# An MoE kernel on one core: turning the first block, the second half of the next up product and the gate are put ahead of the third block's branch and of five weight splits

## The chip, the cores and the metric

The kernel runs on one core of one Trainium2 chip. The time is the device time of one launch in microseconds (us); the kernel before took 2101.19 us in the median of 3 runs (2099.44, 2101.19 and 2105.92). One further execution was taken by the hardware profiler; all rows below are from it.

Names of engines: PE is TensorE's matmul, PEld its weight load, DVE is VectorE, ACT is ScalarE, POOL is GpSimd, and SP is the queue from which the weight transfers are issued. Each works through its instructions in order.

## The reference, cut to what matters

A trunk of two residual layers on 1024 tokens of width 1024, all in float32. Layer 0 mixes tokens with a convolution and an attention, layer 1 with a linear recurrence; neither is touched by the change. Behind each mixer stands a mixture of experts (MoE) with 16 experts, of which each token takes two:

```python
def moe(h2, router_w, router_b, w1, w3, w2):
    ...
    _, loc = lax.top_k(in_group, TOP_K)                  # two experts for each token
    ...
    def run_block(args):
        tok, g, e = args
        xb = h2[tok]                                     # a block of up to 128 tokens of expert e
        y = (jax.nn.silu(xb @ w1[e]) * (xb @ w3[e])) @ w2[e]
        return y * g[:, None]
    ...
    return jnp.zeros_like(h2).at[buf_tok].add(...)
```

w1 and w3 are 1024 x 512 for each expert (the two up products), w2 is 512 x 1024 (the down product). So each layer reads 16 x 6 MB of expert weights, whatever the tokens are.

## The kernel before, in words

**Precision.** Every matrix product is made in three passes. A float32 operand is split into a rounded high part and the rest, both in the matmul's float32 format, and hi x hi, hi x lo and lo x hi are accumulated in one bank (mm3, lines 260 to 264). A product with 128 rows of depth and 512 columns is thus three matmuls; "half of an up product" (four depth steps of eight) is 12 matmuls.

**The weight stream.** The class Ring (lines 60 to 121) brings the weights of the experts in quarters, 128 x 1024 float32 or 512 KB each. SP issues them (line 81) into five tiles named raw (NSTG, line 39). A quarter is then split: ACT copies its high part into a weight slot (line 252), DVE subtracts that from the quarter for the low part (line 253). The raw tile is free for the next issue when both are done. There are four weight slots of four quarters each. The order of the quarters is first w1 and w3 of expert 0, and then for each expert e: w1 of e+1, w2 of e, w3 of e+1. How many quarters are split at which place of the loop stands in one line:

```python
SPLITS = (1, 2, 2, 1, 0, 3, 3)
```

In the loop over expert e (from line 1336) these are: the first quarter of w2 of e (SPLITS[0]); its other three (SPLITS[5], taken ahead of the loop's first branch, emitted in rest_h3); then 2, 2 and 1, which are the four quarters of w3 of e+1 and the first of w1 of e+2 (SPLITS[1] to [3]: the five quarters of the change); and last the other three of w1 of e+2 (SPLITS[6], in second_half). The five quarters go into the slots that w1 and w3 of expert e have held; drop(e, 0) and drop(e, 1) give these slots back. The last reader of these slots is the third or fourth block, inside the branch of line 1410, so the splits wait until PE is past that branch, also where it is skipped.

**Blocks.** Expert e's tokens come as up to four blocks. The first has up to 128 tokens and is always worked. The second is worked where the expert has more: "narrow" with up to 64 further tokens, with a form that needs half the passes (line 1365), or "wide" (line 1355). The third and fourth follow in the branch of line 1410. The branches are taken by a register, some, loaded for each expert on ACT, DVE, PE and POOL (kind: one of five kinds of counts). Rows of tokens are gathered by POOL one and two experts ahead, and the results are scattered by POOL (line 1216).

**The order.** In the expert loops ACT, DVE, PE and POOL run what is written in the order in which it is written (MANUAL, line 43); the transfers on SP are issued where issue() is called, in reload behind the splits. For expert e the order before is:

1. the first half of the w3 product of the first block (h3); the next expert's tokens are turned (prep: transposes on PE, line 1227, copies on ACT, line 1228, subtractions on DVE, line 1229); one split;
2. the branch of the second block: turned tokens, then rest_h3 (second half of h3, the multiplication with the gate, three splits), then the wide or narrow products; without a second block rest_h3 alone;
3. gathers on POOL; the first half of the next expert's w1 product (up1, line 1409);
4. the branch of the third block (line 1410);
5. two splits (line 1420); mid(sF) (line 1421: the first block's gated product is turned by four transposes on PE, line 1245, two ACT copies, line 1247, and two DVE subtractions, line 1248); two splits (line 1422);
6. the second half of up1 and gate_in (lines 1424 and 1425; the gate is one ACT instruction, line 1274); one split (line 1426);
7. the first half of the down product (12 matmuls, line 1430) and its eviction by DVE (line 1256); then, in a branch, the second half with the last three splits, the scatter, and the down products of the further blocks.

A bank of the accumulator is shared between uses: the first half of the first block's down product uses ys[0], and the second half of the second block's uses it again, after DVE has evicted the first (second_half and the lines behind it).

Of the kernel before, what the change touches and what calls it, by code (L numbers as in the profile page):

```python
# [21 lines left out]
KC = D // P  # L22
# [101 lines left out]
class Trunk:  # L124
# [1063 lines left out]
    def moe(self, l):  # L1188
# [48 lines left out]
        def mid(h, ht, n=P, bank=None):  # L1237

            for q in range(2 if bank is None else 1):
                if bank is None:  # L1240
                    js, pt = (2 * q, 2 * q + 1), psX.tile([P, 2, P], F32, name="pht", tag="px")
                else:
                    js, pt = range(4), bank.rearrange("p (j n) -> p j n", j=4)
                for j in js:
                    nc.tensor.transpose(pt[:, j - js[0], 0:n], h[0:n, P * j:P * j + P], self.ident[0:n, 0:n])
                o = slice(js[0], js[-1] + 1)
                nc.scalar.activation(ht[:, 0, o, 0:n], pt[:, :, 0:n], AF.Copy)  # L1247
                nc.vector.tensor_tensor(ht[:, 1, o, 0:n], pt[:, :, 0:n], ht[:, 0, o, 0:n].bitcast(F32),  # L1248
                                        op=ALU.subtract)
# [17 lines left out]
        def up1(e, xt, ks, h1):  # L1267
            mm(h1, xt, weights(e, 0), ks)
# [3 lines left out]
        def gate_in(e, h1):  # L1272
            s = slF[e] = hw.tile([P, FF], F32, name="slF", tag="slF")
            nc.scalar.activation(s, h1, AF.Silu)
# [59 lines left out]
        for e in range(NE):  # L1334
# [71 lines left out]
            if more:  # L1406
                gather_R(e + 1)
                h1 = psH.tile([P, FF], F32, name="h1", tag="h1")
                up1(e + 1, xtF[e + 1], range(4), h1)
            with tc.If(some > 2, preferred_fallthrough_block=False):  # L1410
                prep(rowB, xtR, (r, ys[1]))
                with tc.If(pool_kind(e) > 3):
                    gather(idx[:, c0 + 3:c0 + 4], rowB)
                wide(hx[0])
                with tc.If(some > 3, preferred_fallthrough_block=False):
                    prep(rowB, xtR, (r, ys[1]))
                    wide(hx[1])
            drop(e, 0)
            drop(e, 1)
            split(SPLITS[1])  # L1420
            mid(sF, xt[:, 0])
            split(SPLITS[2])
            if more:
                up1(e + 1, xtF[e + 1], range(4, KC), h1)
                gate_in(e + 1, h1)
            split(SPLITS[3])
            y = rows.tile([P, D], F32, name="y", tag="y")
            gF = gsl[:, c0:c0 + 1]
# [365 lines left out]
```

## Time and profile before

| | |
|---|---|
| median of 3 runs | 2101.19 us (2099.44 to 2105.92) |
| the profiled execution | 2103.05 us; its span 2101.3 us, granted clock 0.937 in the mean |
| busy share of the span | PE 88%, PEld 68%, DVE 66%, ACT 46%, POOL 21% |
| experts of layer 0 | 687.5 to 1171.7 us of the span |
| experts of layer 1 | 1573.8 to 2077.5 us of the span |

Times in rows are microseconds of the span unless they are means, which are in nanoseconds. An engine that is not busy is idle for a reason that the trace infers: "<-DMA raw" means that it waited for a transfer into a tile named raw, "<-PEq L1410" that it waited for a branch or a wait of line 1410 on PE's instruction queue, "<-issue" that nothing that the trace shows held it. Some matmul records are missing from a trace, so counts of matmuls can be a few short. The experts are counted from 0 in each layer. In the trace the bodies of the branches show which expert has which blocks.

### The profile page before, as it was taken

How to read it: one execution, taken by the hardware profiler on the slowest of the kernel's cores; microseconds unless marked ns; L12 is line 12 of the kernel's file. 1: busy time of each engine (PE TensorE's matmuls, PEld its weight loads, DVE VectorE, ACT ScalarE, POOL GpSimd, SP SyncE). 2: the span in 40 equal slices, each digit the busy share in tenths (PEclk: the TensorE clock that was granted, in tenths of full speed). 3: DMA queues.
4: the chain of work that ended last, by engine and by line, in shares of the span. 5: the costliest groups of instructions: out<-in, count | busy, mean ns of one | idle time of the engine just before them, and what ended most of it. 6: DMA issues, size and time to landing. Idle time of an engine off the chain costs nothing. (4 is left out here: it accounts for less than half of the span.)

```text
span 2101.3 us, 27568 instructions
## 1 busy us (share of the span) xinstructions
PE 1850.1 (88%) x9612; PEld 1433.4 (68%) x9612; DVE 1391.2 (66%) x2030; ACT 956.3 (46%) x1332; POOL 432.0 (21%) x264
## 2 busy tenths in 40 slices
PE   5999998998985899989898599999958999887885
PEld 3788575666874677767676478877747777765664
DVE  4599676776679665776756555676785453787772
ACT  3211226665223544555544457782233342565550
POOL 1311104330323111111110232213240110111110
PEclk8999998999986999999999799999979999998897
DMA  8111104677423877897877511124244763999981
GB/s 313 45 57 41 40 1 139 224 260 229 156 99 122 272 227 218 260 305 249 276 212 226 179 33 53 46 71 161 91 150 171 194 203 114 281 307 322 289 286 24
DMA packets 103369, 364.86 MB, mean 174 GB/s; under 512 B 13680, under 2 KB 15024, under 8 KB 103088
## 3 DMA queue, kind: packets, MB, share of 16 engines
q1 hardware_dynamic: 91216, 319.29, 44.8%
q0 software_dynamic: 11776, 41.95, 9.1%
q8 instruction: 157, 2.57, 0.5%
q14 instruction: 124, 1.02, 0.2%
q10 hardware_dynamic: 96, 0.03, 0.0%
HBM read 322.40 MB, written 38.83 MB: 172 GB/s over the span
## 5 line engine op out<-in xcount | busy, mean ns | idle before, releaser
L253 DVE TENSOR_TENSOR wt<-raw,wt 128x1024 fp32r<-128x1024 f32 x384 | 458.7, 1222 | 130.1 <-ACT wt L252 116.5
L252 ACT ACTIVATE wt<-raw 128x1024 fp32r<-128x1024 f32 x384 | 396.9, 1059 | 197.8 <-DMA raw<-in_ex_w_dram 152.3
L262 PE MATMUL h<-wt,xtF 128*128 128x512 f32 x512 | 211.4, 413 | 10.9 <-PEq L1450 5.1
L263 PE MATMUL h<-wt,xtF 128*128 128x512 f32 x512 | 204.5, 399 | 9.5 <-issue 9.5
L264 PE MATMUL h<-wt,xtF 128*128 128x512 f32 x512 | 204.8, 400 | 0.9 <-DVE xtF L1229 0.8
L482 DVE SCALAR_TENSOR_TENSOR cacc<-u,vecs,cacc 128x1024 f32<-128x1024 f32 x116 | 149.5, 1289 | 3.3
L262 PE MATMUL yp<-wt,xtF 128*128 128x512 f32 x256 | 114.7, 448 | 35.9 <-ACT xtF L1247 31.9
L253 POOL TENSOR_TENSOR wl<-raw,wh 128x1024 fp32r<-128x1024 f32 x32 | 85.1, 2678 | 239.6 <-ACT wh L252 232.4
L262 PEld LDWEIGHTS h<-wt,xtF 128*128 128x128 f32 x512 | 98.3, 192 | 32.8 <-issue 10.2
L264 PEld LDWEIGHTS h<-wt,xtF 128*128 128x128 f32 x512 | 98.2, 192 | 30.7 <-issue 6.0
L264 PE MATMUL yp<-wt,xtF 128*128 128x512 f32 x256 | 111.7, 436 | 5.7 <-DVE xtF L1248 4.7
L263 PEld LDWEIGHTS h<-wt,xtF 128*128 128x128 f32 x512 | 98.4, 192 | 26.4 <-issue 7.3
L262 PE MATMUL pout<-wouth,ch 128*128 128x512 f32 x256 | 110.2, 431 | 3.8 <-ACT wouth L252 2.2
L263 PE MATMUL yp<-wt,xtF 128*128 128x512 f32 x256 | 110.2, 431 | 0.0
L1228 ACT ACTIVATE xtF<-pxt 128x512 fp32r<-128x512 f32 x64 | 35.0, 595 | 163.5 <-PE pxt L1227 148.1
L263 PE MATMUL pout<-woutl,ch 128*128 128x512 f32 x256 | 104.1, 407 | 4.0 <-DVE woutl L253 3.4
L264 PE MATMUL pout<-wouth,cl 128*128 128x512 f32 x256 | 103.5, 404 | 0.1
L1216 POOL DMA_INDIRECT xacc<-y,sidx x16 | 33.9, 2121 | 335.7 <-DVE y L1256 312.0
L1216 POOL DMA_INDIRECT out_dram<-y,sidx x16 | 33.8, 2114 | 325.6 <-DVE y L1256 325.6
L262 PEld LDWEIGHTS yp<-wt,xtF 128*128 128x128 f32 x256 | 54.5, 213 | 57.4 <-ACT xtF L1247 36.9
L1526 POOL DMA_INDIRECT xg<-h2d,idx x45 | 58.7, 1305 | 126.0 <-issue 45.5
L1229 DVE TENSOR_TENSOR xtF<-pxt,xtF 128x512 fp32r<-128x512 f32 x64 | 41.2, 685 | 55.8 <-ACT xtF L1228 55.8
(403 smaller groups left out, 4252.0 us busy)
## 6 DMA issues: line engine op xcount, KB each, us to landing
raw<-in_ex_w_dram SPq DMA_DIRECT2D x384, 512.0 KB, 6.0
raw<-in_mod_w_dram SPq DMA_DIRECT2D x96, 512.0 KB, 4.7
raw<-in_ev_w_dram SPq DMA_DIRECT2D x16, 512.0 KB, 4.3
raw<-in_od_in_dram SPq DMA_DIRECT2D x16, 512.0 KB, 5.3
h2d<-x SPq DMA_DIRECT2D x14, 512.0 KB, 2.6
xs<-in_x_dram SPq DMA_DIRECT2D x8, 512.0 KB, 7.7
raw<-in_ev_out_dram SPq DMA_DIRECT2D x8, 512.0 KB, 5.7
x<-in_x_dram SPq DMA_DIRECT2D x8, 512.0 KB, 4.4
```

What stands on the lines that cost most here:

```text
L252: nc.scalar.activation(hi, raw, AF.Copy)
L253: (lo_eng or nc.vector).tensor_tensor(lo, raw, hi.bitcast(F32), op=ALU.subtract)
L262: nc.tensor.matmul(out, ah, bh, start=start, stop=False)
L263: nc.tensor.matmul(out, ah, bl, start=False, stop=False)
L264: nc.tensor.matmul(out, al, bh, start=False, stop=stop)
L482: nc.vector.scalar_tensor_tensor(y if j < CW - 1 else acc[:, c, :], u[:, j:j + S], self.vec("ev_dw_w", 4 * j + c), y, op0=ALU.mult, op1=AL ...
L1216: nc.gpsimd.indirect_dma_start(out=xacc, out_offset=bass.IndirectOffsetOnAxis(ap=col, axis=0), in_=y[0:n], in_offset=None, compute_op=ALU.add)
L1228: nc.scalar.activation(xt[:, q, 0], px, AF.Copy)
L1229: nc.vector.tensor_tensor(xt[:, q, 1], px, xt[:, q, 0].bitcast(F32), op=ALU.subtract)
L1526: self.nc.gpsimd.indirect_dma_start(out=dst, out_offset=None, in_=self.h2d[l], in_offset=bass.IndirectOffsetOnAxis(ap=col, axis=0))
```

## The change

The call mid(sF) and, where there is a next expert, the second half of up1 and gate_in are moved from behind the branch of line 1410 and between the splits to the place directly behind the first half of up1, ahead of that branch. The splits of 2, 2 and 1 quarters, with their reloads, now stand together behind the branch and the two drops. Nothing else is changed; SPLITS, the slots, the five raw tiles and the order of the quarters stay. So on PE the branch of line 1410 and the third block's products now stand between the second half of up1 and the down product; on ACT the two copies of mid and the gate stand ahead of the five splits; on DVE the two subtractions of mid stand ahead of the five subtractions; and SP's five issues stand behind them as before.

```diff
@@ -1407,6 +1407,10 @@
                 gather_R(e + 1)
                 h1 = psH.tile([P, FF], F32, name="h1", tag="h1")
                 up1(e + 1, xtF[e + 1], range(4), h1)
+            mid(sF, xt[:, 0])
+            if more:
+                up1(e + 1, xtF[e + 1], range(4, KC), h1)
+                gate_in(e + 1, h1)
             with tc.If(some > 2, preferred_fallthrough_block=False):
                 prep(rowB, xtR, (r, ys[1]))
                 with tc.If(pool_kind(e) > 3):
@@ -1418,11 +1422,7 @@
             drop(e, 0)
             drop(e, 1)
             split(SPLITS[1])
-            mid(sF, xt[:, 0])
             split(SPLITS[2])
-            if more:
-                up1(e + 1, xtF[e + 1], range(4, KC), h1)
-                gate_in(e + 1, h1)
             split(SPLITS[3])
             y = rows.tile([P, D], F32, name="y", tag="y")
             gF = gsl[:, c0:c0 + 1]
```

## Rows read from the trace of the kernel before

**Rows 1.** From the page: busy time of each engine over the whole span, its share, and the number of instructions.

```profile
PE 1850.1 (88%) x9612; PEld 1433.4 (68%) x9612; DVE 1391.2 (66%) x2030; ACT 956.3 (46%) x1332; POOL 432.0 (21%) x264
```

**Rows 2.** Busy time by windows: the experts of layer 0, those of layer 1, expert 8 of layer 0, and experts 5 to 14 of layer 1. Columns: the window and its length; busy us of PE, PEld, DVE, ACT and POOL, each with its number of instructions; the granted clock of PE; the busy share of the DMA engines; GB/s.

```profile
687.50:1171.70 484.20, 433.88 (x1954) 343.22 (x1952) 308.37 (x349) 239.78 (x308) 71.89 (x45) 0.96 0.80 244
1573.80:2077.50 503.70, 447.06 (x1955) 355.81 (x1954) 308.94 (x342) 238.14 (x298) 69.97 (x42) 0.95 0.74 228
935.50:966.00 30.50, 29.33 (x144) 23.72 (x143) 20.27 (x24) 16.88 (x23) 3.31 (x2) 1.00 0.76 237
1814.80:2051.20 236.40, 199.22 (x842) 155.67 (x840) 181.07 (x191) 143.84 (x170) 35.79 (x20) 0.93 0.93 299
```

**Rows 3.** Instructions of single lines. The first row, by lines: the narrow second block's products (busy us, mean ns, idle before). The others, by source line: the shortest, middle and longest duration in ns, and the first and last start; L1355 is the gate of a wide block (into slR the second, into rowA the third and fourth), L1410 on PEldq the semaphore step on PE's queue where the branch of the third block is skipped.

```profile
L1365 PE MATMUL r<-wt,xtR 128*128 128x512 f32 x144 | 35.1, 395 | 0.1
...
L1355 ACT ACTIVATE slR<-r x4: 597/597/598, 801.9 to 1725.3; 128x512 f32<-128x512 f32 x4
L1355 ACT ACTIVATE rowA<-r x3: 597/598/599, 1607.6 to 1754.9; 128x512 f32<-128x512 f32 x3
...
L1410 PEldq EVENT_SEMAPHORE x30: 51/51/51, 696.4 to 2065.7; - x30
```

**Rows 4.** The table of waits over the whole span: the engine and line that waited, what for, total us, number, longest us.

```profile
ACT wt L252 <- DMA raw<-in_ex_w_dram: 152.3, 145, 4.2
...
ACT wt L252 <- PEq L1410: 35.9, 17, 7.8
PE yp L262 <- ACT xtF L1247: 31.9, 11, 6.4
```

**Rows 5.** The timeline of ACT and PE in expert 6 of layer 0, an expert with one block: start, duration, engine, line, operation, number; in brackets the idle time before it and what ended it.

```profile
896.30 1.06 ACT L252 ACTIVATE wt<-raw 128x1024 fp32r<-128x1024 f32 x1 [3.45 <-DMA raw<-in_ex_w_dram]
...
899.66 1.06 ACT L252 ACTIVATE wt<-raw 128x1024 fp32r<-128x1024 f32 x1 [2.31 <-DMA raw<-in_ex_w_dram]
...
900.63 0.64 ACT L1247 ACTIVATE xtF<-pht 128x256 fp32r<-128x256 f32 x2
901.04 0.65 PE L262 MATMUL yp<-wt,xtF 128*128 128x512 f32 x1 [4.97 <-ACT xtF L1247]
```

**Rows 6.** The timeline of ACT, PE and DVE in expert 8 of layer 0, which has a second block.

```profile
954.28 2.01 ACT L252 ACTIVATE wt<-raw 128x1024 fp32r<-128x1024 f32 x2 [1.60 <-PEq L1410]
954.89 0.63 PE L1245 MATMUL pht<-ident,slF 128*128 128x128 f32 x4 [0.74 <-PEq L1410]
956.20 0.64 ACT L1247 ACTIVATE xtF<-pht 128x256 fp32r<-128x256 f32 x2
957.88 0.39 PE L264 MATMUL h<-wt,xtF 128*128 128x512 f32 x1
958.11 0.40 PE L262 MATMUL yp<-wt,xtF 128*128 128x512 f32 x1
958.32 3.48 DVE L253 TENSOR_TENSOR wt<-raw,wt 128x1024 fp32r<-128x1024 f32 x3
958.87 0.58 ACT L1274 ACTIVATE slF<-h 128x512 f32<-128x512 f32 x1
961.72 0.74 DVE L1256 SCALAR_TENSOR_TENSOR y<-yp,gsl,g2r 128x512 f32<-128x512 f32 x1
970.23 0.75 DVE L1256 SCALAR_TENSOR_TENSOR rowB<-yp,gsl,g2r 128x512 f32<-128x512 f32 x1 [2.05 <-PE yp L264]
```

**Rows 7.** The timeline of ACT and PE at the ends of runs of one-block experts in layer 0: in expert 0 the last split ahead of the copies, the copies, and the first matmul of the down product; then the copies of the next tokens at the starts of experts 1, 8, 11 and 14.

```profile
702.21 1.06 ACT L252 ACTIVATE wt<-raw 128x1024 fp32r<-128x1024 f32 x1 [1.49 <-DMA raw<-in_ex_w_dram]
706.53 0.64 ACT L1247 ACTIVATE xtF<-pht 128x256 fp32r<-128x256 f32 x2
706.95 0.80 PE L262 MATMUL yp<-wt,xtF 128*128 128x512 f32 x1 [6.40 <-ACT xtF L1247]
719.27 1.10 ACT L1228 ACTIVATE xtF<-pxt 128x512 fp32r<-128x512 f32 x2 [3.94 <-PE pxt L1227]
937.94 1.09 ACT L1228 ACTIVATE xtF<-pxt 128x512 fp32r<-128x512 f32 x2 [2.84 <-PE pxt L1227]
1021.21 1.09 ACT L1228 ACTIVATE xtF<-pxt 128x512 fp32r<-128x512 f32 x2 [0.82 <-PE pxt L1227]
1120.06 1.09 ACT L1228 ACTIVATE xtF<-pxt 128x512 fp32r<-128x512 f32 x2 [3.40 <-PE pxt L1227]
```

**Rows 8.** Groups of instructions by line in the window of experts 5 to 14 of layer 1 (1814 to 2051 us): number, busy us, mean ns, idle time before them and what ended it.

```profile
L252 ACT ACTIVATE wt<-raw 128x1024 fp32r<-128x1024 f32 x120 | 124.3, 1058 | 67.5 <-DMA raw<-in_ex_w_dram 63.1 <-PEq L1410 3.1
L1228 ACT ACTIVATE xtF<-pxt 128x512 fp32r<-128x512 f32 x20 | 10.9, 596 | 21.0 <-PE pxt L1227 20.9
L262 PE MATMUL yp<-wt,xtF 128*128 128x512 f32 x80 | 36.3, 454 | 10.3 <-ACT xtF L1247 10.3
L264 PE MATMUL yp<-wt,xtF 128*128 128x512 f32 x80 | 36.0, 450 | 2.5 <-DVE xtF L1248 2.4
```

**Rows 9.** Single rows of timelines: two of the five splits in expert 5 of layer 0, and two places where PE stood with "issue" as the reason, in expert 13 of layer 0 and expert 13 of layer 1.

```profile
873.00 1.06 ACT L252 ACTIVATE wt<-raw 128x1024 fp32r<-128x1024 f32 x1 [1.33 <-PEq L1410]
877.67 1.06 ACT L252 ACTIVATE wt<-raw 128x1024 fp32r<-128x1024 f32 x1 [1.44 <-DMA raw<-in_ex_w_dram]
1108.69 0.59 PE L263 MATMUL h<-wt,xtF 128*128 128x512 f32 x1 [5.41 <-issue]
2014.96 0.59 PE L1245 MATMUL pht<-ident,slF 128*128 128x128 f32 x2 [5.33 <-issue]
```

## The prediction, blind

> **What bounds the kernel now.** I read the page's busy times first, then the table of waits, the windows of the two expert stages, and last the timelines of single experts. TensorE (PE) is busy for 1850.1 us of the 2101.3 us span [rows 1], so where PE has work the order around it can gain little; the change touches the two expert stages alone, 484.2 and 503.7 us, where PE is busy for 433.9 and 447.1 us [rows 2]. The reader should see in [rows 2] that these stages have two kinds of experts. Expert 8 of layer 0 has more than 128 tokens and so a second block: clock 1.00, PE busy 29.33 of 30.5 us, DMA share 0.76. PE is its limit. The ten experts 5 to 14 of layer 1 have one block each: DMA share 0.93 over 236.4 us, clock 0.93, PE busy 199.2 us. The weight transfers are their limit. By the counts, 9 experts have a narrow second block (144 products at 16 each), 4 a wide one, 2 of these a third block; the branch of the third block is skipped 30 times of 32 [rows 3]. So 19 experts have one block. The move of the third block itself concerns 2 experts; what it does to the 30 others is only that copies, up product and gate change places with the split of five weight quarters.
>
> The waits say where these places hurt [rows 4]: PE's down product waited 31.9 us in 11 cases for ScalarE's (ACT) copy of the turned first block (L1247), ACT's splits waited 35.9 us for the branch on PE's queue (L1410), and 152.3 us for weights to land. [rows 5] show the first in expert 6 of layer 0. ACT works in order; the two copies stand behind the splits of two quarters whose data come late (3.45 and 2.31 us of waiting), run at 900.63, and PE starts the down product at 901.04 after 4.97 us idle. The quarters ahead of the copies belong to the next expert's third weight; the down product doesn't need them.
>
> **The change, part by part.** Nothing is added or removed; the same copies, matmuls, splits and transfers run. (a) The four transposes and two copies come right behind the first half of the next up product. (b) The second half of it (12 matmuls) and the gate follow. (c) Then the branch, the five splits with their subtractions on VectorE (DVE), and the issue of five transfers on SP, which still stands behind the branch. (d) The down product follows on PE as before.
>
> What waits newly: the five splits now wait until PE has passed a branch that lies a half up product later, and for the gate on ACT. Behind them on ACT stand the next three splits and the next expert's copies, on DVE five subtractions and the evictions of the down product, on SP five transfers that need their tiles freed. POOL's instructions keep their order; its scatter waits for the second eviction. I price this in an expert with a second block, expert 8 of layer 0 [rows 6]. Today the splits start at 954.28. The up product's second half ends as the down product starts at 958.11; without the branch between (0.74 us at 954.89) it would end at 957.4, the gate (0.58) then runs to about 958.1, and the first split starts near 958.3: 4.0 us later. PE pays the 0.74 us of the branch before the down product instead, so its down product starts at 958.1 again: 0. DVE takes 1.16 us per quarter (3.48 for three), so five end near 965.2, and the first eviction (0.75) near 965.9. PE needs that bank for the second half of the second block's down product: three halves of 12 matmuls at 0.23 us after 958.1 and the next branch's wait, about 967. It fits with about 1 us to spare. DVE is today idle for 2.05 us before its last eviction at 970.23, and that takes up the later start. I take 0 for the 13 experts with a second block; the bounds are 0 and the whole 4.0 us each. In the two with a third block the up product no longer lies behind that block, but the down product needs nothing more from it: 0, bounded by one branch wait (0.74 us) either way.
>
> In experts with one block, the gain is that PE no longer waits for the copies. Where the transfers are the limit, an earlier PE only waits later, so I count only what reaches the end of a run of such experts, where one with a second block begins. There today ACT waits for PE before the copies of the next tokens (L1228), with its weights already landed, and then PE is the limit until the next such run [rows 7].
> - Expert 0 to 1 of layer 0: ACT waits 3.94 us (719.27), because PE was idle for 6.40 us until 706.95. The last quarter that the down product needs is split at 702.21 for 1.06 us, its subtraction ends some 1.2 us later, at 704.5, and the copies can follow the split. PE starts 2.3 us earlier: 2.3.
> - Expert 7 to 8: ACT waits 2.84 us (937.94). This run starts with expert 5, behind one with a second block, where the first of the five splits starts at 873.00 [rows 9] and would start some 4.0 us later, as in expert 8; the stream is behind from there: I take 1.2 of 0 to 2.84.
> - Expert 10 to 11: 0.82 us (1021.21); DVE is busy through it: 0.
> - Expert 13 to 14: 3.40 us (1120.06); DVE's chain of subtractions behind the last landed quarter leaves part of it: 2.0 of 0 to 3.4.
> - The ten experts of layer 1: ACT waits 20.9 us for PE before these copies, PE 10.3 and 2.4 us for the turned block [rows 8]. The DMA share of 0.93 bounds the gain by 0.07 x 236.4 = 16.5 us. Below it is bounded by a loss: each of the five splits waits for the gate, and a quarter held for 4.0 us in expert 4 costs that once. I take 4.5, nearer to nothing, since 63.1 us of the splits' waiting there is for data.
>
> Sum: 2.3 + 1.2 + 2.0 + 4.5 = 10.0 us. The profiled execution took 2103.05 us (2101.3 of span and 1.75 around it) and would come to 2093; it lies 1.86 above the median of the runs, 2101.19, so the timed median comes to 2091.2.
>
> PE also stands for 5.41 us within the up product at 1108.69 and for 5.33 us within the transposes at 2014.96, both put down to "issue", shortly behind the skipped branch [rows 9]; I leave their total unchanged. The Trainium skill (Runtime: NRT & Kernel Launch, Instruction fetch mechanics) states that a taken branch to a target outside the fetched pages makes the engine wait for a fetch. By that rule such a stand moves with the branch to just ahead of the down product, where it holds the down product but no longer the gate; the last one then takes some 2 us of the 4.5, and the sum would be 8. The trace agrees only in that these stands lie behind a branch.
>
> **The rivals.** First, the transfers decide everywhere and PE's lead is spent before each run ends. For it speak the 152.3 us of waiting for data; against it the 3.94, 2.84 and 3.40 us in which ACT waited for PE with data there. It gives about a quarter of the sum, 2.5: 2098.7. Second, slower: the held quarters. Five raw tiles are all there are; held for 4 us, they stop SP's next issues, and where an expert with one block follows one with a second block (experts 5, 9, 13 of layer 0, 4 of layer 1) the stream never makes it up: 4 x 4.0 = 16.0 us of loss against the 10 of gain, 2107.2. It decides from the point at which the next quarters land later than the product that reads them is ready. Against it: at 877.67 and 896.30 the later quarters [rows 5, 9] come so late that the gate would be over first. Third, more: PE's lead frees buffers earlier and the stream of layer 1 closes all of its idle 16.5 us; with the 5.5 of layer 0 that is 22, 2079.2.
>
> **How the numbers follow.** The forecast has 0.47 (its own range 2086 to 2096), the first rival 0.28, the slower one 0.14, the third 0.11. The range 2079 to 2105 reaches to the third and over the first, and leaves out what is slower than that. A measurement of this kernel tells about 0.3%, 6.3 us, from no change. Faster by more has the third and nearly all of the forecast, 0.57; within it the first and the forecast's upper edge, 0.29; slower 0.14.
>
> **What would show it.** In the trace after: the wait of PE's down product for L1247 falls from 31.9 us to under 10; L1247 runs ahead of the fifth to ninth split in each expert; in expert 8 the first of the five splits starts about 4 us later against the down product, which starts with no new wait; the ten experts of layer 1 take 230 to 234 us. The prediction is wrong if experts with a second block grow by more than 1 us each, if the later evictions on DVE delay the second block's down product, or if the ten take as long as before while PE's idle time has only moved.

## The result, and the profile after

The changed kernel took 2128.24 us in the median of 4 runs, the kernel before 2101.24 us beside it: ratio 1.0127, 95% interval 1.0103 to 1.0152. That is 27 us slower, where 10 us faster was forecast and the range ended at 2105. The profiled execution took 2128.80 us, its span 2127.0. Times are medians of executions at the usual granted clock; two executions of over 3000 us at a lower one, one of E10 below and one of the kernel before beside it, are left out.

The busy times of the page of the changed kernel, against [rows 1]:

```profile
PE 1850.2 (87%) x9612; PEld 1424.9 (67%) x9612; DVE 1386.8 (65%) x2030; ACT 963.2 (45%) x1332; POOL 432.5 (20%) x264
```

Over the whole span PE's work is the same to 0.1 us; what was added is idle time. The two expert stages, in the columns of [rows 2]:

```profile
688.80:1183.90 495.10, 435.18 (x1954) 341.38 (x1952) 307.24 (x349) 243.09 (x308) 72.14 (x45) 0.97 0.77 239
1588.50:2102.60 514.10, 445.25 (x1955) 349.63 (x1954) 306.48 (x342) 241.23 (x298) 70.23 (x42) 0.97 0.71 223
```

Layer 0's experts take 495.1 us for 484.2, layer 1's 514.1 for 503.7. So 21.3 us of the 25.7 by which the span grew lie in the two expert stages; the other 4.4 lie outside them, and I did not follow them. The ten one-block experts of layer 1, cut where PE starts expert 5 and where it starts expert 15, take 233.2 us for 233.7, at the same DMA share; the kernel before first, then the changed one:

```profile
1811.80:2045.50 233.70, 199.18 (x842) 155.81 (x841) 178.57 (x189) 141.53 (x169) 35.79 (x20) 0.93 0.94 303
...
1833.50:2066.70 233.20, 196.13 (x841) 149.90 (x840) 176.65 (x188) 146.15 (x170) 34.83 (x20) 0.96 0.94 307
```

To see where the 21.3 come from, the stages are cut where PE starts an expert. First the kernel before: experts 2 to 4 of layer 0 (all with a second block, behind one that has one too), 5 to 8 (three with one block, then one with two), 0 to 3 of layer 1 (all with a second block), 5 to 15 of layer 1 (ten with one block, then one with two).

```profile
752.00:862.70 110.70, 106.10 (x496) 85.19 (x496) 65.37 (x78) 50.17 (x67) 16.23 (x11) 1.00 0.74 219
862.70:970.70 108.00, 94.69 (x416) 74.03 (x416) 75.99 (x84) 59.67 (x74) 15.11 (x10) 0.95 0.88 278
...
1573.00:1789.00 216.00, 202.26 (x922) 163.69 (x921) 103.46 (x122) 76.78 (x103) 29.45 (x19) 0.99 0.59 174
1811.80:2082.30 270.50, 230.40 (x973) 180.78 (x971) 191.52 (x206) 149.25 (x180) 39.36 (x22) 0.92 0.84 267
```

The same stretches of the changed kernel:

```profile
753.80:872.10 118.30, 108.66 (x496) 86.33 (x496) 65.56 (x79) 50.78 (x67) 17.92 (x12) 0.99 0.67 204
872.10:981.80 109.70, 94.64 (x416) 73.50 (x416) 76.21 (x84) 61.24 (x74) 16.96 (x11) 0.97 0.86 275
...
1587.70:1811.90 224.20, 204.03 (x922) 163.57 (x921) 102.66 (x121) 77.75 (x103) 28.13 (x18) 0.99 0.55 166
1833.50:2107.40 273.90, 228.55 (x973) 175.76 (x971) 189.50 (x205) 153.08 (x181) 38.41 (x22) 0.95 0.83 268
```

Seven experts with a second block in a row lose 7.6 and 8.2 us; expert 12 of layer 0, also behind one with a second block, goes from 36.2 to 38.0. Together 17.6 us in eight experts for which I had written 0. The rows with one-block experts lose 1.7 and 3.4, where a gain was forecast; with the stretches left out here (experts 0, 1, 9 to 11 and 13 to 15 of layer 0, 4 of layer 1) this part comes to 3.7. It is the difference of two larger ones, counted from PE's start of an expert to its start of the next: the one-block experts took 14.2 us less, and the five experts with a second block that follow one-block experts (1, 8, 11 and 14 of layer 0, 15 of layer 1) took 17.9 us more. Experts 5 to 7 of layer 0, for example, took 67.0 us for 71.8, and expert 8 behind them 42.7 for 36.2.

The table of waits of the changed kernel (engine and line, what it waited for: us in total, times, longest), against [rows 4]:

```profile
ACT wt L252 <- DMA raw<-in_ex_w_dram: 172.1, 185, 5.1
...
PE yp L262 <- ACTq L1414: 18.2, 25, 0.8
...
PE r L262 <- DVEq L1442: 11.0, 8, 1.5
...
PE yp L262 <- DVEq L1414: 10.4, 4, 6.0
...
PE yp L262 <- issue: 8.8, 3, 4.2
...
PE r L1227 <- issue: 7.1, 2, 4.6
...
PE yp L264 <- issue: 6.7, 3, 3.2
...
PE r L262 <- DVE xtR L1248: 5.3, 4, 2.2
```

The down product's wait for the copies, 31.9 us in [rows 4], is gone; the line has no row any more. In its place the down product waits for the branch (L1414 here, L1410 before); 6.0 us of that are in expert 0 of layer 0, where it had waited 6.4 us for the copies. And r<-wt,xtR, the second block's down product, waits for DVE: in eight narrow experts at line 1442, 11.0 us, and in the four wide ones for the subtraction of their own mid (xtR, line 1248), 5.3 us. Neither row existed before. The four wide experts and four of these narrow ones are the eight that lost 17.6 us; 10.6 us of that are these waits.

Expert 8 of layer 0 in the changed kernel, ACT, PE and DVE from three timelines, against [rows 6]:

```profile
967.72 4.86 ACT L252 ACTIVATE wt<-raw 128x1024 fp32r<-128x1024 f32 x5 [0.33 <-ACTq L1414]
...
967.50 0.47 PE L262 MATMUL yp<-wt,xtF 128*128 128x512 f32 x1 [0.74 <-ACTq L1414]
970.97 0.49 PE L262 MATMUL yp<-wt,xtF 128*128 128x512 f32 x1 [0.43 <-PEq L1442]
975.45 0.48 PE L262 MATMUL r<-wt,xtR 128*128 128x512 f32 x1 [1.41 <-DVEq L1442]
...
968.82 5.77 DVE L253 TENSOR_TENSOR wt<-raw,wt 128x1024 fp32r<-128x1024 f32 x5 [3.81 <-ACT wt L252]
974.50 0.75 DVE L1256 SCALAR_TENSOR_TENSOR y<-yp,gsl,g2r 128x512 f32<-128x512 f32 x1
```

Read it against the start of the down product, 967.50. The first split starts 0.2 us behind it (3.8 ahead in [rows 6]: 4.0 us later, as forecast), the five subtractions end 7.1 us behind it (forecast 7.1), the first eviction starts 7.0 us behind it (3.6 before). All this is as the working said. What it did not say is the row at 975.45: PE has finished both halves of the first block's down product and stands for 1.41 us, until DVE, behind its eviction, passes the branch of line 1442. That branch holds mid of a wide second block. One source line's instructions show why it matters where it is skipped (shortest, middle, longest ns, first and last start):

```profile
L1442 DVEq EVENT_SEMAPHORE  x9: 21/21/21, 747.4 to 2099.1; - x9
```

Nine times, once in each narrow expert, DVE gives a semaphore as it passes the skipped branch. In the code the body that it skips reads the bank r and writes xtR on DVE, and the next matmul, r<-wt,xtR, writes r and reads xtR. That this semaphore stands for the skipped work is my reading of the two; that PE waits for it is the row. In a wide expert the body runs, and PE waits at the same place for its result.

### The profile page after: what moved, and what is told of

Read it like the earlier page. It is cut to its first block, busy times and chain, and to the rows that moved or that the text cites. A ratio compares the mean times of both kernels' runs of the same rounds, so it can differ in the third digit from the quotient of the medians.

```text
span 2127.0 us, 27566 instructions
## 1 busy us (share of the span) xinstructions
PE 1850.2 (87%) x9612; PEld 1424.9 (67%) x9612; DVE 1386.8 (65%) x2030; ACT 963.2 (45%) x1332; POOL 432.5 (20%) x264
## 5 line engine op out<-in xcount | busy, mean ns | idle before, releaser
L262 PE MATMUL h<-wt,xtF 128*128 128x512 f32 x512 | 216.6, 423 | 26.2 <-ACT xtF L1228 9.0
L264 PE MATMUL h<-wt,xtF 128*128 128x512 f32 x512 | 208.5, 407 | 7.4 <-DVE xtF L1229 7.2
L263 PE MATMUL h<-wt,xtF 128*128 128x512 f32 x512 | 206.3, 403 | 0.2 <-issue 0.2
L262 PE MATMUL yp<-wt,xtF 128*128 128x512 f32 x256 | 109.1, 426 | 45.4 <-ACTq L1414 18.2
L262 PEld LDWEIGHTS h<-wt,xtF 128*128 128x128 f32 x512 | 100.4, 196 | 57.7 <-issue 18.6
L264 PEld LDWEIGHTS h<-wt,xtF 128*128 128x128 f32 x512 | 99.6, 194 | 35.7 <-DVE xtF L1229 13.1
L263 PEld LDWEIGHTS h<-wt,xtF 128*128 128x128 f32 x512 | 100.2, 196 | 19.8 <-issue 0.6
L264 PE MATMUL yp<-wt,xtF 128*128 128x512 f32 x256 | 104.5, 408 | 6.7 <-issue 6.7
L263 PE MATMUL yp<-wt,xtF 128*128 128x512 f32 x256 | 104.4, 408 | 2.6 <-issue 2.6
L262 PEld LDWEIGHTS yp<-wt,xtF 128*128 128x128 f32 x256 | 50.1, 196 | 71.0 <-ACTq L1414 29.9
L277 PE MATMUL pm<-raw,condb 128*32 128x256 f32 x768 | 59.2, 428 | 20.3 <-DMA raw<-in_mod_w_dram 15.2
```

The costliest lines, as they stand in the source:

```text
L262: nc.tensor.matmul(out, ah, bh, start=start, stop=False)
L263: nc.tensor.matmul(out, ah, bl, start=False, stop=False)
L264: nc.tensor.matmul(out, al, bh, start=False, stop=stop)
L277: nc.tensor.matmul(pm[32 * g:32 * g + 32, 0:256], self.condb[:, k, :], raw[k // 4][:, g, :], start=k < 4, stop=k >= 4)
```

## The experiments

Each run is timed against runs of the kernel before on the same chip; a time is the median, behind it the ratio with its 95% interval. Runs are E1 to E14. The diffs are against the changed kernel where nothing else is said.

**E1: mid alone ahead of the branch.**

```diff
             mid(sF, xt[:, 0])
-            if more:
-                up1(e + 1, xtF[e + 1], range(4, KC), h1)
-                gate_in(e + 1, h1)
             with tc.If(some > 2, preferred_fallthrough_block=False):
...
             split(SPLITS[2])
+            if more:
+                up1(e + 1, xtF[e + 1], range(4, KC), h1)
+                gate_in(e + 1, h1)
             split(SPLITS[3])
```

> Only the turning of the first block (mid) is put ahead of the third block's branch; the second half of the up product and the gate stay behind the splits of 2 and 2 quarters, as before. Theory DVE: the loss comes from the five subtractions, which start 4 us later and stand on DVE right ahead of the down product's evictions, so that PE waits for DVE at the branch of the second block. Here the splits start as early as in the kernel before: PE's wait for DVE at that branch is under 2 us in total (11.0 in the changed kernel), a narrow second-block expert takes 36.0 to 36.6 us (37.9 to 39 in the changed kernel), and the gain of the one-block experts stays: 2086 to 2093 us. Theory mid: if the earlier turning itself did the harm, the time stays above 2115. Theory tiles (weights held longer in the five raw tiles): as theory DVE here, 2086 to 2095.

Measured: 2096.16 us, 0.9974 (0.9957 to 0.9991). The same four stretches:

```profile
749.70:860.40 110.70, 106.51 (x496) 85.69 (x496) 65.25 (x78) 50.40 (x67) 19.46 (x11) 1.00 0.72 218
860.40:969.50 109.10, 94.22 (x416) 74.45 (x417) 75.89 (x84) 60.98 (x74) 18.04 (x11) 0.95 0.86 277
...
1574.40:1790.60 216.20, 202.83 (x922) 164.04 (x921) 103.10 (x121) 77.53 (x103) 26.67 (x18) 0.99 0.58 173
```

Experts with a second block in a row are back at 110.7 and 216.2 us, and the waits for DVE at line 1442 and for mid of the wide experts have no row. So the loss of the 17.6 us comes from the up product and the gate, not from mid. But the gain was half of what I expected: 5 to 8 still takes 109.1 us for 108.0. Its PE waits and two rows of timelines (PE and DVE, expert 8) show what takes it:

```profile
PE r L1227 <- issue: 21.4, 5, 5.5
```

```profile
935.48 1.09 PE L1227 MATMUL r<-ident,xg 128*128 128x128 f32 x4 [5.01 <-issue]
...
934.64 0.75 DVE L1256 SCALAR_TENSOR_TENSOR y<-yp,gsl,g2r 128x512 f32<-128x512 f32 x1
```

PE comes to the second block's transposes 5.0 us early and stands; they start 0.1 us after DVE has ended an eviction (934.64 + 0.75 = 935.39). "issue" means here only that the trace saw no releaser. That eviction is the one of expert 7's second half, and it stands on DVE behind subtractions whose quarters land late; E5 shows below that it need not be the eviction that ends such a stand. What one-block experts win, the first second-block expert behind them gives back.

**E2: the gate put back behind the branch and four splits.**

```diff
-                gate_in(e + 1, h1)
...
             split(SPLITS[2])
+            if more:
+                gate_in(e + 1, h1)
             split(SPLITS[3])
```

> The changed kernel with the gate alone put back behind the branch and four of the five splits; mid and the second half of the up product stay ahead. Theory DVE: the splits still wait for PE to pass the branch behind the up product, so they start at most 0.7 us earlier against the down product; PE's wait for DVE at the second block's branch stays at 5 to 14 us in total, the time at 2115 to 2126. Theory branch: the loss is PE's wait for ACT, which passes the branch only behind the gate (about 0.74 us in each of some 25 experts ahead of the down product, 18.2 us in total); that wait falls under 4 us and the time to 2104 to 2112. Theory tiles: the quarters are held 0.7 us less, 2122 to 2128.

Measured: 2117.99 us, 1.0090 (1.0073 to 1.0107). In expert 12 of layer 0 (PE; the profiled execution, 2105.79 us, was the fastest of its runs by 12 us, so its waits may be short):

```profile
1090.09 0.48 PE L262 MATMUL r<-wt,xtR 128*128 128x512 f32 x1 [0.56 <-DVEq L1443]
```

Both theories were off by a little. The wait for ACT at the branch went, but PE now waits 10.9 us there for its own queue, 0.75 us a time, and 22.2 us for DVE (10.4 in the changed kernel), so theory branch gains nothing by it. The wait for DVE fell from 11.0 to 4.0 us, just under the band of theory DVE; the gate ahead of the splits had been worth more than half of it.

**E3: shorter work on DVE.** The five quarters' subtraction becomes a copy of the high part.

```diff
         nc.scalar.activation(hi, raw, AF.Copy)
+        if short:
+            return nc.vector.tensor_copy(lo, hi)
```

> The changed kernel in which the five quarters get a plain DVE copy of the high part in place of the subtraction (their low part is left out of the result). ACT's splits, the branch and the order stay. Theory DVE: if the copy is shorter than 1.15 us, DVE ends its five about 1.2 us earlier (ACT's last split is then what holds it), PE's wait at the second block's branch falls from 11.0 to under 4 us, and the time to 2104 to 2116. Theory branch: 2122 to 2130, the 0.74 us each stay. Theory tiles: the tiles come free 0.5 us earlier, 2118 to 2128.

Measured: 2080.22 us, 0.9910 (0.9878 to 0.9942). Since layer 0's output differs, layer 1's tokens go to other experts; only layer 0 can be compared. It takes 483.4 us (684.8 to 1168.2) for 495.1 in the changed kernel. In expert 12:

```profile
1078.32 0.69 DVE L254 CAST wt<-wt 128x1024 fp32r<-128x1024 f32 x1 [3.86 <-ACT wt L252]
...
1082.73 0.74 DVE L1258 SCALAR_TENSOR_TENSOR y<-yp,gsl,g2r 128x512 f32<-128x512 f32 x1
```

The copy takes 0.69 us for 1.22, the eviction comes 1.3 us earlier against the down product, and PE's wait for DVE at the branch has no row of its own. ACT, the branch and the order are as in the changed kernel. 11.7 us in one layer by DVE's length alone: theory DVE, and more than it expected, since the one-block experts gain too. The shorter copies also free the raw tiles earlier; how much of the one-block experts' gain is due to that, this run does not show.

**E4: two of the five subtractions behind the second block's branch**, ACT's copies where they were.

```diff
-            split(SPLITS[1])
-            split(SPLITS[2])
-            split(SPLITS[3])
+            split(3)
+            ps5 = take(2)
+            emit(ps5, part=1)
...
             def second_half():
+                emit(ps5, part=2)
                 ps2 = emit(ps, 2)
```

> The changed kernel in which DVE's subtractions of the last two of the five quarters are put behind the branch of the second block, ahead of the last three; ACT's copies stay where they are, and the two raw tiles are held longer and issued again later. Theory DVE: DVE evicts the first half and reaches the second block's branch 2.3 us earlier, PE's wait there falls from 11.0 to under 3 us and the time to 2108 to 2118. Theory tiles: two tiles are held 2 us longer, so the time rises to 2130 to 2145. Theory branch: 2125 to 2132.

Measured: 2156.01 us, 1.0252 (1.0228 to 1.0276). The wait for DVE at the branch is gone, as theory DVE had it, and the time rose all the same, as theory tiles had it. Rows of its waits:

```profile
ACT wt L253 <- DMA raw<-in_ex_w_dram: 211.1, 203, 5.6
...
PE r L1367 <- ACT wt L253: 15.3, 5, 3.9
```

ACT waits 39 us longer for data than in the changed kernel, and PE waits for ACT, which stands behind a split, in the narrow second block. So raw tiles held longer do cost, some 28 us net for two tiles here. In the changed kernel this does not show: experts 5 and 9 of layer 0, behind ones with a second block, took 19.8 and 19.3 us, for 19.8 and 19.6 before, expert 13 of layer 0 24.1 for 26.4, and expert 4 of layer 1 21.6 for 22.9.

**E5, E6 and E7: the eviction of the second half first, in one-block experts.** E5 is E1 with this edit, E7 the changed kernel with it; E6 is E5 with SPLITS (1, 2, 2, 0, 1, 3, 3), the fifth split behind the first half of the down product.

```diff
-            def second_half():
-                ps2 = emit(ps, 2)
+            def second_half(n):
+                ps2 = emit(ps, n)
...
-                second_half()
+                second_half(2)
...
             with second.Else():
-                second_half()
+                second_half(0)
```

> The kernel of the run with mid alone moved, and in experts with one block DVE evicts the second half of the down product ahead of the last three subtractions, no longer behind two of them. Theory eviction: the one-block experts' gain was given back where a second block follows, because PE's transposes there need a bank whose eviction stood behind subtractions of late quarters (21.4 us of PE idle time ahead of r<-ident in that run, five places); two quarters less in front take 2 to 3 us off each: that idle time falls under 12 us and the time to 2083 to 2091. Theory stream: the transfers give the pace and PE's lead ends in another wait (for weights, L252): 2093 to 2099.

> The run before this, and the fifth of the five splits is put behind the first half of the down product, so that DVE evicts that half behind four subtractions. Theory eviction: the first eviction comes one quarter earlier (1.2 us or the wait for its data), 1 to 2 us less at each of the five places: 2079 to 2088, PE's idle time ahead of r<-ident under 8 us; experts with a second block stay within 0.3 us, since DVE has the same work ahead of their branch. Theory stream: 2093 to 2099.

> The changed kernel with the same eviction first in experts with one block. Theory DVE in two parts: (1) the wait at the second block's branch is untouched, 9 to 13 us for r<-wt,xtR on DVE; (2) the entry into a second block after one-block experts gains 1 to 2.5 us at five places: 2116 to 2123 us. Theory stream: 2125 to 2131.

Measured: E5 2090.93 us, 0.9949 (0.9932 to 0.9967); E6 2090.38, 0.9951 (0.9932 to 0.9970); E7 2122.31, 1.0091 (1.0055 to 1.0126). Rows of the waits, E5 and then E7:

```profile
PE yp L262 <- DVEq L1411: 29.6, 13, 5.8
PE r L1227 <- issue: 9.7, 4, 4.0
```

```profile
PE r L262 <- DVEq L1442: 10.7, 8, 1.4
```

In E5 the wait ahead of the second block's transposes falls from 21.4 to 9.7 us, and the time is 5 us below E1's, with intervals that overlap; but the down product's wait for DVE at line 1411, the branch of the third block, rises from 10.7 to 29.6 us. In E6 the first wait falls to 2.6 us and the second stays at 28.8; the time doesn't fall further and lies above E6's band. In E7 the wait at line 1442 stays (10.7 for 11.0) and that at line 1414 rises from 10.4 to 37.0 us; the time is 6 us below the changed kernel's, again with intervals that overlap.

Theory eviction has its numbers in E5, but not its mechanism. Expert 8 of layer 0 in E5, DVE and PE:

```profile
928.60 1.41 DVE L1256 SCALAR_TENSOR_TENSOR y<-yp,gsl,g2r 128x512 f32<-128x512 f32 x2
929.92 2.35 DVE L253 TENSOR_TENSOR wt<-raw,wt 128x1024 fp32r<-128x1024 f32 x2
...
932.37 1.01 PE L1227 MATMUL r<-ident,xg 128*128 128x128 f32 x4 [4.01 <-issue]
```

Both evictions of expert 7 have ended at 930.01, and PE stands on until 932.37, 0.1 us after the second subtraction behind them has ended. In E1 it goes on 0.1 us after the eviction of the second half, which stands behind two subtractions. In both this is the third instruction of DVE behind the eviction of the first half, and so it is at each of these stands in E1, E5 and the changed kernel. I read it as a wait for DVE's place in its queue, as at line 1442; which data it stands for I can't show. That these stands got shorter because PE was held longer ahead of the down product is my reading of the two waits; where E5's few us come from stays open. E1, E5, E6, E12 and E13 beat both kernels, by 0.3 to 0.5% against the kernel before; which of them is best their intervals don't tell.

**E8: two of the five subtractions on POOL**, so that DVE has three.

```diff
-            split(SPLITS[1])
-            split(SPLITS[2])
+            split(SPLITS[1], self.nc.gpsimd)
+            split(SPLITS[2], self.nc.gpsimd)
```

(the second argument is the engine of the last subtraction of the two)

> The changed kernel with the subtractions of the second and fourth of the five quarters on POOL, whose subtraction of that size took 2.7 us against 1.2 on DVE, so no raw tile comes free earlier. Theory DVE: DVE comes to the first eviction some 2 us earlier, PE's wait at the second block's branch falls from 11.0 to under 3 us, and a narrow second-block expert that follows another takes 36.2 to 37.0 us (37.9 to 39.0 in the changed kernel): 2104 to 2117 us. Theory tiles: the tiles are held as long or longer, 2126 to 2145.

Measured: 2173.67 us, 1.0344 (1.0313 to 1.0374). Expert 12 of layer 0, PE and DVE:

```profile
1122.83 0.48 PE L262 MATMUL r<-wt,xtR 128*128 128x512 f32 x1 [3.60 <-DVEq L1442]
...
1115.98 5.99 DVE L253 TENSOR_TENSOR wt<-raw,wt 128x1024 fp32r<-128x1024 f32 x2 [0.67 <-ACT wt L252]
1121.89 0.74 DVE L1256 SCALAR_TENSOR_TENSOR y<-yp,gsl,g2r 128x512 f32<-128x512 f32 x1
```

The edit failed at its purpose: two subtractions on DVE took 5.99 us beside those on POOL, and DVE was not earlier but later. PE followed it: 3.60 us of waiting for 1.39 in this expert. The number of theory tiles was passed too, and by another way than it says.

**E9 and E10: which part makes E5's gain.** E9 is the kernel before with the eviction first and nothing else; E10 has mid behind the branch and ahead of the splits as well.

```diff
+            mid(sF, xt[:, 0])
             split(SPLITS[1])
-            mid(sF, xt[:, 0])
             split(SPLITS[2])
```

> The kernel before with the eviction of the second half ahead of the last three subtractions in one-block experts, and nothing else. Theory eviction: in the kernel before PE waited for the copies of the first block, so it was not early, and its evictions were not behind late quarters: no gain, 2098 to 2105 us, and the gain of the run that has both comes from the earlier turning. If the order of the eviction alone makes the gain: 2088 to 2095.

> The kernel before with two steps: mid stands directly behind the third block's branch and the drops, ahead of the five splits' first two, and the eviction first in one-block experts. Theory DVE: what counts is that mid stands ahead of the splits and that the splits are not held back; where the branch stands does not matter: 2088 to 2095, as in the run with mid ahead of the branch and eviction first. Theory branch (the gain needs mid ahead of the branch): 2095 to 2102.

Measured: E9 2112.39 us, 1.0048 (1.0029 to 1.0068); E10 2100.01, 0.9995 (0.9971 to 1.0018). E9 is worse than no gain: PE's wait for the copies rose from 31.9 to 46.3 us. By the code the eviction first holds two raw tiles until PE's half is done; that this comes back to PE where mid stands behind two splits is my reading of the two numbers. Mid ahead of the splits brings 12 us on top (E10), and E10 stands 9 us behind E5, as theory branch said. Why mid ahead of the branch is worth so much I can't show; it stays open.

**E11: the splits behind the gate, the branch where it was** (against the kernel before).

```diff
-            split(SPLITS[1])
             mid(sF, xt[:, 0])
-            split(SPLITS[2])
             if more:
...
+            split(SPLITS[1])
+            split(SPLITS[2])
             split(SPLITS[3])
```

> The kernel before with the branch of the third block left where it was, and only the five splits put behind mid, the second half of the up product and the gate. Theory DVE: the loss hangs on the splits' place, not on the branch's: DVE's first eviction starts 6.9 to 7.8 us behind the start of the down product in a narrow expert that follows another (4.0 before, 7.0 in the changed kernel), PE waits there 1.4 to 2.2 us each time, 10 to 20 us in all, and the time is 2118 to 2134. Theory branch (the branch right ahead of the down product does it): PE finds no branch there, 2088 to 2104.

Measured: 2150.56 us, 1.0225 (1.0183 to 1.0267). Expert 12, PE:

```profile
1108.58 0.48 PE L262 MATMUL r<-wt,xtR 128*128 128x512 f32 x1 [1.96 <-DVEq L1442]
```

With no branch ahead of the down product the loss is there and larger, so it is the splits' place that does it. The wait is in the forecast band, here and in all (15.5 us); the time lies 17 us above its upper end. By PE's starts the eight experts lose 28.0 us (17.6 in the changed kernel) and the five behind one-block experts 34.3 (17.9); I have not followed why.

**E12, E13 and E14.** E12 and E14 are E1 and the changed kernel with SPLITS (1, 2, 2, 0, 1, 3, 3); E13 is E5 with second_half(1) in the one-block case.

> The run with mid alone moved, and only the fifth split put behind the first half of the down product (no eviction first). Theory eviction: the first eviction stands behind one quarter less, PE's idle time ahead of r<-ident falls by 1 to 2 us at each of five places against the run with mid alone, without holding a raw tile longer: 2086 to 2093 us. Theory stream: 2093 to 2099.

> The run with mid moved and the eviction first, but with one of the last three subtractions ahead of the eviction in one-block experts (two in the run with mid alone, none in the run with eviction first). The eviction alone, without mid, cost 11 us, by raw tiles held longer; half of that order should cost less and keep most of the entry's gain: 2086 to 2092 us. If the entry alone counts, it lies between the two runs, 2091 to 2096.

> The changed kernel with the fifth split put behind the first half of the down product, so DVE evicts that half behind four subtractions, and the fifth follows ahead of the branch. If PE waits for DVE's arrival at the second block's branch: the wait stays at 1.2 to 1.6 us in a narrow expert that follows another, 9 to 13 us in all, and the time at 2118 to 2130. If PE waits for the eviction itself: 0.2 to 0.4 us each, under 4 us in all, 2104 to 2116.

Measured: E12 2095.66 us, 0.9958 (0.9942 to 0.9973); E13 2093.05, 0.9951 (0.9930 to 0.9972); E14 2130.37, 1.0116 (1.0097 to 1.0135). E12 and E13 settle little: the wait ahead of the transposes is 12.4 us in both (21.4 in E1), and their times can't be told from E1's or E5's. E14 settles what PE waits for. Expert 12, PE and DVE:

```profile
1091.97 0.47 PE L262 MATMUL yp<-wt,xtF 128*128 128x512 f32 x1 [0.76 <-ACTq L1414]
...
1099.90 0.48 PE L262 MATMUL r<-wt,xtR 128*128 128x512 f32 x1 [1.39 <-DVEq L1442]
...
1097.82 0.75 DVE L1256 SCALAR_TENSOR_TENSOR y<-yp,gsl,g2r 128x512 f32<-128x512 f32 x1
```

The eviction comes 1.15 us earlier than in the changed kernel (5.85 us behind the down product's start for 7.00), and PE waits 1.39 us as before, 11.2 us in all. It is not the eviction that PE needs but DVE's arrival at the branch, with all five subtractions done.

**One table of all.** Expert 12 of layer 0 has a narrow second block and follows another; no data are late in it. Times from the timelines of each kernel; the last column is from PE's start of this expert to its start of the next.

| kernel | down product starts | first eviction starts | later by | PE's wait for DVE | expert |
|---|---|---|---|---|---|
| before | 1077.75 | 1081.70 | 3.95 | 0 | 36.2 |
| E1 | 1078.24 | 1082.28 | 4.04 | 0 | 36.1 |
| E3 | 1077.02 | 1082.73 | 5.71 | 0.1 | 36.7 |
| E2 | 1082.99 | 1089.14 | 6.15 | 0.56 | 37.2 |
| changed | 1090.55 | 1097.55 | 7.00 | 1.39 | 38.0 |
| E11 | 1100.17 | 1107.63 | 7.46 | 1.96 | 38.4 |
| E8 | 1112.70 | 1121.89 | 9.19 | 3.60 | 41.6 |

From 5.6 us on, each us that DVE is later is a us of PE's waiting (from E2 to E8: 3.04 us later, 3.04 more). From E2 to E11 the expert grows by 0.3 to 0.4 us more than the wait, in E8 by 1.8. E14 is not in the table: there the fifth subtraction stands behind the eviction, and the wait goes by the subtraction.

## Why the prediction was wrong, point by point

**The step that failed** is "I take 0 for the 13 experts with a second block". Its working was right up to its last line. Splits 4.0 us later: 4.0. PE pays the branch before the down product instead (0.74): 0.74. Five subtractions end and the first eviction follows: to 0.1 us. Then "PE needs that bank for the second half of the second block's down product, ... about 967. It fits with about 1 us to spare." PE needs DVE half a down product earlier, ahead of the second block's first half, and not for a bank but at the branch of line 1442 (11.0 us) or, in the wide experts, for what that branch's body writes (5.3 us). The timeline that [rows 6] are taken from had the sign, in DVE's next subtraction:

```profile
962.86 2.49 DVE L253 TENSOR_TENSOR wt<-raw,wt 128x1024 fp32r<-128x1024 f32 x2 [0.40 <-DVEq L1442]
```

DVE stood 0.40 us for line 1442, in an expert that skips that branch. I took a skipped branch on DVE for free. Of the upper bound, "the whole 4.0 us each", eight experts came to 1.6 to 4.2 us, 17.6 in all, 2.2 each; the five behind one-block experts lost 1.7 to 6.6. That bound was named and then left out of the range. Of the signs of being wrong that the text names, two came as written: experts with a second block grew by more than 1 us each, and the ten experts of layer 1 took as long as before.

A part of the loss is not idle time: in experts 2 to 4 PE's busy time rose from 106.1 to 108.7 us for the same 496 instructions, with the granted clock at 0.99 for 1.00; in experts 0 to 3 of layer 1 it rose from 202.3 to 204.0. It is gone together with the stands in E1, where experts 2 to 4 are busy for 106.5.

**The one-block experts.** That the copies would no longer hold the down product was right. The ten experts of layer 1 took 233.2 us, within "230 to 234", but by the same cut they had taken 233.7 before: that the number fits is luck. In layer 0 the lead came, 2.5 us in expert 0 and 4.8 in experts 5 to 7. That it reaches the end of the run was wrong: "e0 to 1, 2.3", "e7 to 8, 1.2", "e13 to 14, 2.0" and the 4.5 of layer 1 came out, in the same order and each with the expert behind, as losses of 0.5, 1.7, 0.6 and 3.4; experts 10 and 11, written as 0, lost 2.0. The entry rows show why, expert 8 of the changed kernel, DVE and PE:

```profile
944.20 1.22 DVE L253 TENSOR_TENSOR wt<-raw,wt 128x1024 fp32r<-128x1024 f32 x1 [0.36 <-ACT wt L252]
945.34 0.74 DVE L1256 SCALAR_TENSOR_TENSOR y<-yp,gsl,g2r 128x512 f32<-128x512 f32 x1
...
946.19 0.63 PE L1227 MATMUL r<-ident,xg 128*128 128x128 f32 x4 [2.46 <-issue]
```

PE goes on 0.1 us after an eviction that stands behind a subtraction behind late data. ACT's waiting for PE's transposes in [rows 7], on which I built these terms, was the sign that PE was late there; I did not ask what stood on DVE ahead of the place that PE waits for next. E1 shows this stand at five entries, and E5 that it need not be an eviction that ends it. Of the 17.9 us that the five entries lost, another 5.7 are the wait at line 1442, in experts 1, 8, 11 and 14 of layer 0.

**The rivals.** The first (the transfers decide) is what became of the ten experts of layer 1: their pace did not change. In layer 0 it did, and the next expert with a second block gave it back. The slower one had the sign and the wrong place: quarters held for longer do starve the stream (E4), but in the changed kernel the four experts that it named did not get longer. None of the rivals had DVE's queue in it, though the text itself named "on DVE five subtractions and the evictions" as what is queued behind the wait.

**The stands at "issue".** In [rows 9] PE stood within the up product or the transposes, shortly behind the skipped branch. After the change such stands lie in the down product, 8.8 and 6.7 us in the table of waits, and the gate is ahead of them. By the rule of the Trainium skill (Runtime: NRT & Kernel Launch, Instruction fetch mechanics), that a taken branch out of the fetched pages waits for a fetch, they would move with the branch; the trace agrees with that. What they cost in the sum was not tried by itself.

**What held.** With the first loss taken away by leaving the up product where it was (E1), and with the evictions first (E5), the kernel is 10.3 us faster than before, near the 10.0 of the sum, but it is not those terms that came true: E5's stretch of experts 5 to 8 takes 108.1 us, as before, and its 5 to 15 of layer 1 268.0 for 270.5.

```profile
858.30:966.40 108.10, 94.62 (x417) 75.36 (x417) 76.58 (x84) 60.29 (x74) 16.27 (x10) 0.95 0.87 279
...
1804.60:2072.60 268.00, 227.84 (x973) 175.66 (x971) 194.55 (x208) 152.99 (x184) 39.02 (x22) 0.96 0.86 277
```

## What to carry to other kernels

When an edit delays work on an in-order engine, list every later place of that engine for which another engine waits, the skipped branches among them: here a branch that was not taken still had its place in DVE's queue, and PE waited until DVE had come by. Price the delay at the first of these, not at the one that the data flow suggests. And follow a lead to its end: an engine that gets ahead comes sooner to the next place where it waits for another engine, and what stands ahead of that place may be waiting for late data.

## What the runs showed of the hardware

The subtractions of E8 slow each other. One source line's instructions in E8 (shortest, middle, longest ns):

```profile
L253 DVE TENSOR_TENSOR wt<-raw,wt x324: 1206/1221/3426, 649.3 to 2121.4; 128x1024 fp32r<-128x1024 f32 x162
...
L253 POOL TENSOR_TENSOR wt<-raw,wt x60: 2348/2436/3400, 702.7 to 2114.3; 128x1024 fp32r<-128x1024 f32 x60
```

In the changed kernel, with none on POOL beside them, the longest of DVE's took 1.29 us; here up to 3.43 us, as if it had waited for one on POOL to end first. The Trainium skill (SBUF — State Buffer, Who interferes with whom) says that a DVE instruction with two inputs in SBUF contends with a GpSimd instruction that reads SBUF, and that contention on the ports that the two share is an exclusive lock. This subtraction has two such inputs, and the trace agrees: 3.43 is a little under the 1.22 and 2.44 of the two middle values together. I had counted on two engines side by side.
